# Padding the low key halves to 128 rows, a planner that keeps TensorE in one mode, and values of two units in one 512-column projection

## The chip, the cores and the metric

The kernel runs on one core of one Trainium2 chip. The metric is the device time of one execution in microseconds (us). The program is one launch; its inputs are the packed weights and tables, its output the final hidden state.

## The reference

Two layers of an encoder with 512 tokens of width 1024. Each layer normalises `x`, projects it with one wide matrix `w_in`, runs three branches on the pieces, and merges them:

```python
h = rms_norm(x, norm_w[i])
(qa, ka, va, ga, qb, kb, vb, gb, xbc, z, dt_raw, ua, ub, uc) = [h @ w for w in jnp.split(w_in[i], split_idx, axis=1)]
ya = neighbourhood_attention(qa, ka, va, na_rpb[i])   # 16 heads of 64, windows of 8 rows x 16 columns on a 8 x 64 grid
ya = (ya * jax.nn.silu(ga)) @ w_oa[i]
yb = dilated_mixture(rotary(qb), rotary(kb), vb)      # 24 heads in 3 groups of dilation 1, 4, 16, mixed by their log-sum-exp
yb = (yb * jax.nn.silu(gb)) @ w_ob[i]
yc = mamba2_bidirectional(xbc, z, dt_raw, ...) @ w_oc[i]   # 24 heads, chunks of 128, both directions
merged = jax.nn.sigmoid(ua) * ya + jax.nn.sigmoid(ub) * yb + jax.nn.sigmoid(uc) * yc
x = x + merged @ w_out[i]
gate = jax.nn.sigmoid(rms_norm(x, ple_norm_w[i]) @ w_ple_gate[i])
x = x + (p[i] @ w_ple[i]) * gate
```

The last line of the reference is `rms_norm(x, final_norm_w)`. All arithmetic is float32.

## The kernel before

**Precision.** TensorE multiplies in a reduced float32 format (`F32R`), so every operand of a projection is split into a high and a low part: `whi` and `wlo` for weights, `hh` and `hl` for the hidden state. `mm3` makes one product of three matmuls (high-high, high-low, low-high). A weight block of 128 x 1024 is fetched into `raw` by the SP queue; `block` makes `whi` on ScalarE and `wlo` on VectorE. Buffers: three each of `raw`, `whi`, `wlo`.

**Units.** `run` walks a list of steps in `ORDER`: `N0` to `N3` are the neighbourhood attention in units of four heads (`na_unit`), `S0` to `S3` the state-space groups of three head pairs (`ssm_group`, `ssm_pair`), `O0` and `O1` the two halves of the product with `w_oc` (`out_c`), `G` the gate on it, `D0` and `D1` the dilated attention in halves (`dil_half`), `A` and `B` the merges, `L` some stores. Then comes `tail`.

**Scores.** `stack` puts a head's query high part and low part on top of each other in `qs` (128 rows: 64 high, 64 low), and its key high part twice in `ks`; the key's low part goes into `kl`, where the heads of a pair hold 64 rows each. `scores` then needs, per head and half, one matmul `sc<-ks,qs` over 128 rows and one `sc<-kl,qs` over the head's own 64 rows. There are 192 of each. After the softmax, `turn` transposes the probabilities (`tr`), and matmuls into `av` multiply them with the values; an output there has 64 columns a head, in float32, which the profile shows as two passes.

**Values.** `vproj` projects 256 value columns with matmuls of 256 columns and two `pj` banks. `vproj_wide` does 512 columns with four banks (two `pj`, one `tr`, the one `av`); before, only `dil_half` uses it. `na_unit` writes the values to a scratch tensor `vd` and gathers windows of it into `vw`. PSUM has 3 `pj`, 2 `sc`, 2 `tr` banks and 1 `av` bank.

**What sets the order.** The code records all instructions as nodes, in the order of the steps. `schedule` then plans every engine's queue with a list planner: it takes the ready node with the lowest number on each engine, as far as 2500 nodes ahead of the first open one, if its tiles fit into the pools (`fits`), and it prices nodes by `cost`. The order that results is what the engines run; each runs its queue in order. All instructions are issued from one line of `emit` (L261 in the profile of before), so groups in the profile are told apart by the names of tiles.

Of the kernel before, what the change touches and what calls it, by code (L numbers as in the profile page):

```python
# [120 lines left out]
class Node:  # L121
    __slots__ = ("i", "eng", "method", "args", "kw", "tiles", "pred", "succ", "cost", "new", "dma", "table", "fetch", "issue",
                 "npred", "ready", "done", "rank")
# [27 lines left out]
def cost(n, eng):  # L151
# [11 lines left out]
    if eng == "tensor":  # L163
        if n.method == "transpose":
            return 107.0
        if lazy[1].base.dtype == F32R:
            return (0.418 * free + 13.5) * (0.6 if lazy[1].box[0][1] == 64 else 1.0)
        if out.box[0][1] <= 64:
            return 54.0 if out.box[0][0] >= 64 else 1.72 * max(free, 64)
        if lazy[1].box[0][1] == 64:  # L170
            return 240.0
# [21 lines left out]
class Recorder:  # L193
# [28 lines left out]
    def add(self, eng, method, args, kw):  # L222
        n = Node()
        n.i, n.eng, n.method, n.args, n.kw = len(self.nodes), eng, method, args, kw
        n.dma = method == "dma_start"
        n.fetch = n.dma and isinstance(kw["out"], Lazy) and kw["out"].base.pool.space != "DRAM"
# [8 lines left out]
        for group, wr in ((rest, False), (outs, True)):  # L235
            for ap in group:
# [11 lines left out]
                h.append((n, ap.box, wr))  # L248
        n.issue = 625.0 if n.dma and any(scattered(v) for v in (kw["out"], kw["in_"])) else 450.0
# [4 lines left out]
        self.nodes.append(n)  # L254

# [7 lines left out]

    WINDOW = 2500
    AHEAD = 600

    def schedule(self):
# [16 lines left out]
        seen = set()  # L284
        for n in nodes:
            n.new = []
            n.npred = len(n.pred)
            n.ready = 0.0
            for m in n.pred:
                m.succ.append(n)  # L290
            for t, wr in n.tiles.items():
                t.left += 1
                if t not in seen:
                    seen.add(t)
                    if t.tag:
                        n.new.append(t)
        avail = {q: [] for q in self.QUEUE}
        wait = {q: [] for q in self.QUEUE}
        for n in nodes:
            if n.npred == 0:  # L300
                for e in FLEX.get(n.eng, (n.eng,)):
                    heapq.heappush(avail[e], n.i)
# [3 lines left out]
        table, drain = None, False  # L306
# [3 lines left out]
        while len(order) < len(nodes):  # L310
# [3 lines left out]
            for q in avail:  # L314
# [3 lines left out]
                while w and w[0][0] <= now:  # L318
                    heapq.heappush(av, heapq.heappop(w)[1])
                skipped, n = [], None  # L320
                while av:
                    i = av[0]
                    if i > front + self.WINDOW:
# [4 lines left out]
                    if not (nodes[i].dma and i > front + self.AHEAD) and self.fits(nodes[i], free, front):  # L328
                        n = nodes[i]
# [4 lines left out]
                for i in skipped:  # L334
                    heapq.heappush(av, i)
# [7 lines left out]
                for t in n.new:  # L343
                    free[t.tag] -= 1
                    self.live[t.tag][front:n.i] += 1
# [8 lines left out]
                else:  # L354
# [37 lines left out]
    def fits(self, n, free, front):  # L392

        if not n.new:
            return True
        need = {}
        for t in n.new:
            need[t.tag] = need.get(t.tag, 0) + 1
        for k, v in need.items():
            if free[k] < v or (front < n.i and self.live[k][front:n.i].max() + v > self.caps[k]):  # L400
                return False
        return True

# [9 lines left out]
class Emit:  # L413
# [18 lines left out]
    NT = 55  # L432
# [17 lines left out]
    def block(self, spec, ncols):  # L450
# [5 lines left out]
        nc.scalar.copy(hi[:, :ncols], raw[:, :ncols])  # L456
        nc.vector.tensor_sub(lo[:, :ncols], raw[:, :ncols], hi.bitcast(F32)[:, :ncols])
# [42 lines left out]
    def vproj_wide(self, cols):  # L500
# [76 lines left out]
    def constants(self):  # L577
# [15 lines left out]
        self.eps = c(C_EPS, 1)  # L593

# [41 lines left out]
    def norm_h(self):  # L636
# [7 lines left out]
        for k in range(8):  # L644
# [4 lines left out]
            nc.scalar.copy(self.hh[k][:, S:576], self.hh[k].bitcast(F32)[:, 0:64])  # L649
            nc.scalar.copy(self.hl[k][:, S:576], self.hl[k].bitcast(F32)[:, 0:64])  # L650
# [236 lines left out]
    def dil_half(self, hf):  # L887
# [4 lines left out]
        far = self.vproj_wide([VB + 512 * g + 256 * hf for g in (1, 2)])  # L892
# [76 lines left out]
    def scores(self, pair, q, k, kl):  # L969


# [421 lines left out]
```

## Time and profile before

| | |
|---|---|
| median of three runs | 2452.09 us (2450.15 to 2454.11) |
| profiled execution | 2453.53 us, span 2451.6 us |
| mean granted TensorE clock | 0.982 |
| busy: TensorE, VectorE, ScalarE, GpSimd | 2350.0, 1642.3, 1122.5, 215.0 us |
| TensorE instructions | 12480 |
| HBM traffic | 272.74 MB, 111 GB/s mean |

The span is the time from the first to the last instruction of the profiled execution. PE is TensorE's matmuls, PEld its weight loads, DVE VectorE, ACT ScalarE, POOL GpSimd, SP the queue that fetches weights. A name such as `pj<-hh,whi` reads: out `pj`, moving operand `hh`, stationary operand `whi`. The form `64*128 64x256` means 64 rows and 128 columns of the array, and 256 columns that move. Matmuls overlap in the pipeline, so the recorded duration of one is longer than the step from its start to the next one's.

### The profile page before, as it was taken

Reading aid. Unit: us, or ns where it says so; the run is one execution under the profiler, and the core shown is the slowest. Engines: PE = TensorE matmul, PEld = TensorE weight load, DVE = VectorE, ACT = ScalarE, POOL = GpSimd, SP = SyncE. Lnnn points to the kernel's source line nnn. Section 1 sums busy time; section 2 is a strip of 40 time slices with the busy share of each in tenths; the row PEclk is TensorE's granted clock in tenths of the full one; section 3 lists DMA queues with packets and bytes.
Section 4 is the critical chain, followed back from the end, with each engine's and each line's share of the span. In section 5 each row is a group of like instructions: output and inputs, shape, how many; then the busy total and the mean of one; then the engine's idle time right before and its main releaser. Section 6 shows DMA issues by size and latency. Waiting matters only on the chain. (4 is left out here: it accounts for less than half of the span.)

```text
span 2451.6 us, 33345 instructions
## 1 busy us (share of the span) xinstructions
PE 2350.0 (96%) x12480; PEld 1928.1 (79%) x12480; DVE 1642.3 (67%) x3227; ACT 1122.5 (46%) x2148; POOL 215.0 (9%) x380
## 2 busy tenths in 40 slices
PE   7999899989998999999999998999899989999998
PEld 6677788878877877788877777788788778777888
DVE  6797978784465556535687878797735663665357
ACT  5636354433355445324465453644234554562245
POOL 1202020000001000200021110210000020002000
PEclk9999999999999999999999999999999999999999
DMA  6625252423214221533355442523322242116333
GB/s 229 162 88 164 86 149 76 136 80 103 86 61 104 89 78 61 172 116 105 109 170 145 117 142 90 148 88 113 101 93 71 73 124 76 66 61 170 107 110 129
DMA packets 111377, 272.74 MB, mean 111 GB/s; under 512 B 39360, under 2 KB 45984, under 8 KB 111216
## 3 DMA queue, kind: packets, MB, share of 16 engines
q1 hardware_dynamic: 56464, 189.73, 23.4%
q0 software_dynamic: 50400, 76.69, 11.8%
q10 hardware_dynamic: 4352, 4.20, 0.5%
q8 instruction: 98, 1.61, 0.3%
q14 instruction: 63, 0.52, 0.1%
HBM read 257.08 MB, written 13.21 MB: 110 GB/s over the span
## 5 line engine op out<-in xcount | busy, mean ns | idle before, releaser
L261 PE MATMUL pj<-hh,whi 128*128 128x512 f32 x1744 | 700.4, 402 | 3.8 <-ACT hh L261 3.8
L261 PE MATMUL pj<-hl,whi 128*128 128x512 f32 x1744 | 700.7, 402 | 1.4 <-DVE hl L261 1.4
L261 PE MATMUL pj<-hh,wlo 128*128 128x512 f32 x1728 | 693.1, 401 | 8.6 <-DVE wlo L261 8.6
L261 ACT CAST whi<-raw 128x1024 fp32r<-128x1024 f32 (+2 forms) x360 | 368.1, 1024 | 702.2 <-PE pj L261 545.2
L261 DVE TENSOR_TENSOR wlo<-raw,whi 128x1024 fp32r<-128x1024 f32 (+2 forms) x358 | 425.7, 1191 | 377.5 <-ACT whi L261 372.5
L261 PEld LDWEIGHTS pj<-hl,whi 128*128 128x128 f32 x1744 | 330.6, 190 | 79.9 <-issue 8.8
L261 PEld LDWEIGHTS pj<-hh,whi 128*128 128x128 f32 x1744 | 331.0, 190 | 78.4 <-issue 7.0
L261 PEld LDWEIGHTS pj<-hh,wlo 128*128 128x128 f32 x1728 | 326.9, 189 | 83.5 <-DVE wlo L261 10.2
L261 PE MATMUL pj<-yh,wlo 128*128 128x512 f32 (+1 forms) x576 | 213.3, 372 | 0.6 <-DVE wlo L261 0.6
L261 PE MATMUL pj<-yl,whi 128*128 128x512 f32 (+1 forms) x576 | 212.7, 370 | 0.0
L261 PE MATMUL pj<-yh,whi 128*128 128x512 f32 (+1 forms) x576 | 211.9, 369 | 0.6 <-ACT th L261 0.6
L261 PE MATMUL pj<-whi,hh 128*128 128x256 f32 (+1 forms) x448 | 139.4, 314 | 11.0 <-ACT th L261 7.1
L261 PE MATMUL pj<-wlo,hh 128*128 128x256 f32 (+1 forms) x448 | 139.7, 313 | 6.6 <-DVE wlo L261 6.6
L261 PE MATMUL pj<-whi,hl 128*128 128x256 f32 (+1 forms) x448 | 138.2, 311 | 0.0
L261 PEld LDWEIGHTS pj<-yh,wlo 128*128 128x128 f32 x576 | 109.9, 191 | 19.8 <-DVE wlo L261 1.4
L261 PEld LDWEIGHTS pj<-yh,whi 128*128 128x128 f32 x576 | 109.6, 190 | 18.6 <-ACT th L261 1.5
L261 PEld LDWEIGHTS pj<-yl,whi 128*128 128x128 f32 x576 | 109.5, 190 | 17.9 <-issue 0.3
L261 DVE SCALAR_TENSOR_TENSOR cv<-cx,cwh,cv 128x510 f32<-128x510 f32 (+1 forms) x160 | 119.3, 746 | 5.5 <-ACT cv L261 4.2
L261 PEld LDWEIGHTS pj<-whi,hh 128*128 128x128 f32 x448 | 96.0, 215 | 15.9 <-ACT th L261 8.4
L261 PEld LDWEIGHTS pj<-wlo,hh 128*128 128x128 f32 x448 | 97.5, 218 | 9.3 <-DVE wlo L261 8.3
L261 ACT ACTIVATE p<-p,nm 128x128 f32<-128x128 f32 (+2 forms) x192 | 80.1, 420 | 39.6 <-DVE nm L261 39.6
L261 PEld LDWEIGHTS pj<-whi,hl 128*128 128x128 f32 x448 | 97.4, 218 | 0.5 <-issue 0.3
(214 smaller groups left out, 3476.5 us busy)
## 6 DMA issues: line engine op xcount, KB each, us to landing
raw<-wt SPq DMA_DIRECT2D x322, 512.0 KB, 3.3
nb<-nab POOLq DMA_DIRECT2D x32, 384.0 KB, 4.6
af<-acd POOLq DMA_DIRECT2D x48, 256.0 KB, 6.0
ab<-acd POOLq DMA_DIRECT2D x48, 256.0 KB, 6.2
raw<-wt SPq DMA_DIRECT2D x32, 384.0 KB, 3.0
eb<-ead POOLq DMA_DIRECT2D x48, 192.0 KB, 9.6
vw<-vd POOLq DMA_DIRECT2D x56, 128.0 KB, 5.0
f<-fd POOLq DMA_DIRECT2D x24, 256.0 KB, 12.8
```

The costliest lines, as they stand in the source:

```text
L261: getattr(getattr(self.real, n.eng), n.method)(*[f(a) for a in n.args], **{k: f(v) for k, v in n.kw.items()})
```

## The change

Seven edits come together.

1. `kl` becomes a tile per head of 128 rows (`keylow`, two fixed pairs used in turn) whose other 64 rows are zeroed once. `scores` multiplies it over 128 rows, with the same `qs` as for `ks`, and finishes one head before the next.
2. `na_unit` projects the values of two units together with `vproj_wide` in the even unit; `vproj_wide` takes the tokens as an argument.
3. `ORDER` has `N3` between `S3` and `O1`, where it stood between `D0` and `D1`.
4. The planner gives each TensorE node a mode (`half` for 64 rows, `pair` for 64-column outputs, `wide` for the reduced format, `full` for float32). It looks past up to `STAY` = 12 ready nodes of another mode for one of the present mode, if that one is at most `NEAR` = 60 numbers behind.
5. The nodes are taken by rank: the two splits of a weight block count as 300 numbers earlier (`EARLY`), readers of PSUM on other engines as 60 earlier (`DRAIN`). The planner's prices for some matmuls and for a change of mode differ.
6. The copies of the first 64 columns of `hh` and `hl` to their end move from `norm_h` to the step `L` (`stores`).
7. The pool of general tiles has 51 buffers instead of 55; four tiles of that size are the `keylow`.

```diff
-            return (0.418 * free + 13.5) * (0.6 if lazy[1].box[0][1] == 64 else 1.0)
+            return 111.0 if lazy[1].box[0][1] == 64 else 0.418 * free + 13.5
...
-            return 240.0
+            return 136.0
...
+        n.split = False
+        n.drain = eng != "tensor" and any(isinstance(v, Lazy) and v.base.pool.space == "PSUM"
+                                          for v in list(args) + list(kw.values()))
...
+        n.mode = None
+        if eng == "tensor":
+            w = args[1]
+            n.mode = ("half" if w.box[0][1] == 64 else "pair" if args[0].box[0][1] == 64 else
+                      "wide" if w.base.dtype == F32R else "full")
...
+        return n
...
+    EARLY = 300
+    DRAIN = 60
+    STAY, NEAR = 12, 60
...
+            n.rank = n.i - (self.EARLY if n.split else self.DRAIN if n.drain else 0)
...
-                    heapq.heappush(av, heapq.heappop(w)[1])
-                skipped, n = [], None
+                    i = heapq.heappop(w)[1]
+                    heapq.heappush(av, (nodes[i].rank, i))
+                skipped, n, held, tries = [], None, [], 0
...
-                    i = av[0]
-                    if i > front + self.WINDOW:
+                    r, i = av[0]
+                    if r > front + self.WINDOW:
...
-                        n = nodes[i]
+                        if q == "tensor" and nodes[i].mode != mode and tries < self.STAY:
+                            if n is None or nodes[i].rank < n.rank:
+                                n = nodes[i]
+                            tries += 1
+                            held.append(i)
+                            continue
+                        if n is None or nodes[i].mode == mode and r < n.rank + self.NEAR:
+                            n = nodes[i]
+                        else:
+                            held.append(i)
...
-                for i in skipped:
-                    heapq.heappush(av, i)
+                for i in skipped + [i for i in held if n is None or i != n.i]:
+                    heapq.heappush(av, (nodes[i].rank, i))
...
-                        half = n.cost in (54.0, 1.72 * 128)
-                        c += 84.0 if drain and not half else 0.0
-                        drain = half
+                        c += 0.0 if n.mode == mode else 45.0 if {n.mode, mode} == {"wide", "full"} else 95.0
+                        mode = n.mode
...
-    NT = 55
+    NT = 51
...
-        nc.scalar.copy(hi[:, :ncols], raw[:, :ncols])
-        nc.vector.tensor_sub(lo[:, :ncols], raw[:, :ncols], hi.bitcast(F32)[:, :ncols])
+        for n in (nc.scalar.copy(hi[:, :ncols], raw[:, :ncols]),
+                  nc.vector.tensor_sub(lo[:, :ncols], raw[:, :ncols], hi.bitcast(F32)[:, :ncols])):
+            n.split = True
...
-    def vproj_wide(self, cols):
+    def vproj_wide(self, cols, tokens):
...
-                    lh, ll = self.hh[k][:, t:S:4], self.hl[k][:, t:S:4]
+                    lh, ll = self.hh[k][:, tokens[t]], self.hl[k][:, tokens[t]]
...
+        self.nkey = 0
+        self.keylow = [[self.cp.tile([128, S], F32R, name=f"kl{i}_{h}") for h in range(2)] for i in range(2)]
+        for pair in self.keylow:
+            for h in range(2):
+                self.nc.gpsimd.memset(pair[h].bitcast(F32)[64 - 64 * h:128 - 64 * h], 0.0)
...
-            nc.scalar.copy(self.hh[k][:, S:576], self.hh[k].bitcast(F32)[:, 0:64])
-            nc.scalar.copy(self.hl[k][:, S:576], self.hl[k].bitcast(F32)[:, 0:64])
...
 
-
         nc = self.nc
...
                 nc.tensor.matmul(sc[h][:, ii], q(h, pair, ii), k(h, pair, ii), start=ii == 0, stop=False)
-        for ii in range(2):
-            for h in range(2):
-                own = slice(64 * h, 64 * h + 64)
-                nc.tensor.matmul(sc[h][:, ii], q(h, pair, ii)[own], kl(pair, ii, own), start=False, stop=ii == 1)
+            for ii in range(2):
+                nc.tensor.matmul(sc[h][:, ii], q(h, pair, ii), kl(h, pair, ii), start=False, stop=ii == 1)
         return sc
...
-                             lambda b, ii, own: kl[own, keys(2 * b + ii)])
+                             lambda h, b, ii: kl[h][:, keys(2 * b + ii)])
...
         nc = self.nc
-        vn = self.vproj("w_in", VA + 256 * u, [slice(128 * t, 128 * t + 128) for t in range(4)])
-        vd = self.dp.tile([S, 256], F32, tag="vd", bufs=2, name=self.name("vd"))
-        for j in range(2):
-            nc.scalar.dma_start(out=vd[256 * j:256 * j + 256].rearrange("(t p) d -> p t d", p=128), in_=vn[j])
-        vg = vd.rearrange("(r c) d -> r c d", c=64)
+        if u % 2 == 0:
+            vn = self.vproj_wide([VA + 256 * u, VA + 256 * u + 256], [slice(128 * t, 128 * t + 128) for t in range(4)])
+            self.vd = self.dp.tile([S, 512], F32, tag="vd", bufs=2, name=self.name("vd"))
+            for t in range(4):
+                nc.scalar.dma_start(out=self.vd[128 * t:128 * t + 128], in_=vn[t].rearrange("p g d -> p (g d)"))
+        vg = self.vd.rearrange("(r c) d -> r c d", c=64)[:, :, 256 * (u % 2):256 * (u % 2) + 256]
         V = {}
...
-        kl = self.t(dtype=F32R, nm="kl")
+        kl = self.keylow[self.nkey % 2]
+        self.nkey += 1
...
-                eng.tensor_sub(kl[a], kp[a], ks[h].bitcast(F32)[a])
+                eng.tensor_sub(kl[h][a], kp[a], ks[h].bitcast(F32)[a])
...
-                nc.vector.scalar_tensor_tensor(kl[a], kp[a], scale, ks[h].bitcast(F32)[a], ALU.mult, ALU.subtract)
+                nc.vector.scalar_tensor_tensor(kl[h][a], kp[a], scale, ks[h].bitcast(F32)[a], ALU.mult, ALU.subtract)
...
+        nc = self.nc
+        for h in self.hh + self.hl:
+            nc.scalar.copy(h[:, S:576], h.bitcast(F32)[:, 0:64])
...
-    ORDER = ("N0 L S0 N1 S1 N2 S2 O0 S3 O1 G D0 N3 D1 A B",
-             "N0 L S0 N1 S1 N2 S2 O0 S3 O1 G D0 N3 D1 A B")
+    ORDER = ("N0 L S0 N1 S1 N2 S2 O0 S3 N3 O1 G D0 D1 A B",
+             "N0 L S0 N1 S1 N2 S2 O0 S3 N3 O1 G D0 D1 A B")
```

Three places show what that does to the order. The names in the rows are out<-moving,stationary for TensorE and out<-inputs elsewhere; the last column is the shape of the out, and buffer numbers are part of the names.

First, TensorE in N0 of the first layer, at the outputs of the first pair's second half. Before:

```order
L261 MATMUL pj_786<-hl_283,whi_596 128x512
L261 MATMUL pj_786<-hh_270,wlo_613 128x512
L261 MATMUL av_798<-pt_829,vw_559 64x128
L261 MATMUL pj_786<-hh_281,whi_596 128x512
L261 MATMUL av_798<-pt_838,vw_559 64x128
L261 MATMUL av_798<-pt_829,vw_602 64x128
L261 MATMUL av_798<-pt_838,vw_602 64x128
L261 MATMUL av_798<-pt_829,vw_578 64x128
L261 MATMUL av_798<-pt_838,vw_578 64x128
L261 MATMUL av_798<-pt_829,vw_578 64x128
L261 MATMUL av_798<-pt_838,vw_578 64x128
L261 MATMUL pj_786<-hl_289,whi_596 128x512
```

And now:

```order
L270 MATMUL pj_802<-hh_320,whi_651 128x512
L270 MATMUL av_853<-pt_887,vw_625 64x128
L270 MATMUL av_853<-pt_893,vw_625 64x128
L270 MATMUL av_853<-pt_887,vw_665 64x128
L270 MATMUL av_853<-pt_893,vw_665 64x128
L270 MATMUL av_853<-pt_887,vw_646 64x128
L270 MATMUL av_853<-pt_893,vw_646 64x128
L270 MATMUL av_853<-pt_887,vw_646 64x128
L270 MATMUL av_853<-pt_893,vw_646 64x128
L270 MATMUL pj_802<-hl_356,whi_651 128x512
```

The eight outputs stood as one and seven with a projection between them, and now stand together. Over the whole program the stretches of `av` outputs of 64 columns number 191 before and 149 now, of which those of a single output 89 and 66 (others of seven: 69 and 63); stretches of transposes number 254 and 225, single ones 126 and 84. The 192 matmuls `sc<-kl` stand in 68 stretches of two and 14 of four before.

Second, TensorE at the last head pair of S3 in the first layer; `tr<-consts,cv` is its transpose, `sc<-cx` the first matmul on the result, `pj<-yh` and `pj<-yl` are O1's projections. Before:

```order
L261 MATMUL pj_4828<-yl_3863,whi_4800 128x512
L261 MATMUL tr_4837<-consts_114,cv_4764 128x128 x4
L261 MATMUL sc_4861<-cx_4857,tT_4442 128x128 x3
L261 MATMUL sc_4866<-cx_4859,tT_4442 128x128 x3
L261 MATMUL pj_4812<-yh_3851,wlo_4868 128x512
L261 MATMUL pj_4812<-yh_4044,whi_4661 128x512
```

Now the transpose stands 17 projection rows of N3 ahead of `sc<-cx`; the last of them and what follows:

```order
L270 MATMUL pj_4775<-hh_315,whi_4632 128x512
L270 MATMUL pj_4775<-hl_351,whi_4632 128x512
L270 MATMUL pj_4775<-hh_315,wlo_4649 128x512
L270 MATMUL sc_4819<-cx_4812,tT_4413 128x128 x3
L270 MATMUL sc_4826<-cx_4816,tT_4413 128x128 x3
L270 MATMUL pj_4775<-hh_320,whi_4632 128x512
```

N3's projections `pj<-hh` and `pj<-hl` now fill the place that was empty between the two. For all 24 head pairs of the S groups the projections between the transpose and `sc<-cx` number 0 to 12 before and 7 to 17 now.

Third, VectorE behind D0 in the first layer, where D0's outputs `o` are multiplied with factors `f` that come back from a scratch tensor. Before, N3's low keys stand among them:

```order
L261 TENSOR_TENSOR o_5957<-o_5957,f_6875 128x512
L261 TENSOR_TENSOR wlo_6914<-raw_6832,whi_6901 128x1024
L261 TENSOR_TENSOR o_6057<-o_6057,f_6885 128x512
L261 SCALAR_TENSOR_TENSOR kl_6934<-pj_6853,ks_6912 64x512
L261 TENSOR_TENSOR o_5957<-o_5957,o_6057 128x512
```

Now it is D1 that follows, and its blocks stand there:

```order
L270 TENSOR_TENSOR wlo_7229<-raw_7004,whi_7221 128x1024
L270 TENSOR_TENSOR o_6331<-o_6331,f_7236 128x512
L270 TENSOR_TENSOR wlo_7270<-raw_7195,whi_7260 128x1024
L270 TENSOR_TENSOR o_6437<-o_6437,f_7244 128x512
L270 TENSOR_TENSOR o_6584<-o_6584,f_7251 128x512
L270 TENSOR_TENSOR o_6331<-o_6331,o_6437 128x512
```

`wlo_7229` is the last low half of D1's far values, ahead of the first product with `f`; `wlo_7270`, behind it, is the block that D1 needs after them. No low key stands between the products any more.

More of the change, by code (lines that the diff above doesn't have):

```diff
@@ L121 @@
 class Node:
-    __slots__ = ("i", "eng", "method", "args", "kw", "tiles", "pred", "succ", "cost", "new", "dma", "table", "fetch", "issue",
-                 "npred", "ready", "done", "rank")
+    __slots__ = ("i", "eng", "method", "args", "kw", "tiles", "pred", "succ", "cost", "dma", "table", "fetch", "issue",
+                 "npred", "ready", "done", "rank", "split", "drain", "mode")
 LATENCY = {"PE": {"PE": 0.0, "*": 197.0}, "ACT": {"ACT": 63.0, "PE": 271.0, "POOL": 159.0, "*": 142.0},
@@ L283, in schedule @@
         assert not over, over
-        seen = set()
+        self.first, self.placed = first, set()
         for n in nodes:
-            n.new = []
             n.npred = len(n.pred)
+            n.rank = n.i - (self.EARLY if n.split else self.DRAIN if n.drain else 0)
             n.ready = 0.0
@@ L292, in schedule @@
                 t.left += 1
[L293 to L296, printed above, removed]
         avail = {q: [] for q in self.QUEUE}
@@ L301, in schedule @@
                 for e in FLEX.get(n.eng, (n.eng,)):
-                    heapq.heappush(avail[e], n.i)
+                    heapq.heappush(avail[e], (n.rank, n.i))
         clock = dict.fromkeys(self.QUEUE, 0.0)
@@ L305, in schedule @@
         dge = dma = now = 0.0
-        table, drain = None, False
+        table, mode = None, None
         events, order = [], []
@@ L342, in schedule @@
                 n.cost = cost(n, q)
-                for t in n.new:
+                for t in self.new(n):
+                    self.placed.add(t)
                     free[t.tag] -= 1
-                    self.live[t.tag][front:n.i] += 1
+                    self.live[t.tag][front:first[t]] += 1
                 if n.dma:
@@ L392, in fits, with new @@
     def fits(self, n, free, front):
[L394 to L397, printed above, removed]
+        need, until = {}, {}
+        for t in self.new(n):
             need[t.tag] = need.get(t.tag, 0) + 1
+            until[t.tag] = max(until.get(t.tag, 0), self.first[t])
         for k, v in need.items():
-            if free[k] < v or (front < n.i and self.live[k][front:n.i].max() + v > self.caps[k]):
+            if free[k] < v or (front < until[k] and self.live[k][front:until[k]].max() + v > self.caps[k]):
                 return False
         return True
+    def new(self, n):
+        return [t for t in n.tiles if t.tag and t not in self.placed]
 class RecEngine:
@@ L891, in dil_half @@
         near = self.vproj("w_in", VB + 256 * hf, [slice(64 + 128 * t, 192 + 128 * t) for t in range(4)])
-        far = self.vproj_wide([VB + 512 * g + 256 * hf for g in (1, 2)])
+        far = self.vproj_wide([VB + 512 * g + 256 * hf for g in (1, 2)], [slice(t, S, 4) for t in range(4)])
         val = lambda g, t: far[t][:, g - 1] if g else near[t // 2][:, t % 2]
@@ L1150, in na_pair @@
             sc = self.scores(b, lambda h, b, jj: q[h][:, 256 * b + 128 * jj:256 * b + 128 * jj + 128],
-                             lambda h, b, jj: win(k[h], 2 * b + jj), lambda b, jj, own: win(kl[own], 2 * b + jj))
+                             lambda h, b, jj: win(k[h], 2 * b + jj), lambda h, b, jj: win(kl[h], 2 * b + jj))
             mx = self.small((128, 2, 2), "nmx")
```

## The prediction

> **What bounds the kernel now.** I read the page first: the span, the busy time of each engine. TensorE is the bound.
>
> ```profile
> span 2451.6 us, 33345 instructions
> PE 2350.0 (96%) x12480; PEld 1928.1 (79%) x12480; DVE 1642.3 (67%) x3227; ACT 1122.5 (46%) x2148; POOL 215.0 (9%) x380
> ```
>
> So PE idles 2451.6 - 2350.0 = 102 us, and a gain has to come out of that or out of the 2350. The view of PE's waits comes next (engine, line, who is waited for: total us, times, longest). Short waits on VectorE lead it, among them one on the low key tile `kl` and one on `cx` of an S group; the 9.3 is the first load.
>
> ```profile
> PE pj L261 <- DVE wlo L261: 15.8, 13, 3.4
> PE sc L261 <- DVE kl L261: 12.6, 4, 5.1
> PE pj L261 <- ACT whi L261: 9.3, 1, 9.3
> PE sc L261 <- DVE cx L261: 8.5, 6, 3.2
> ```
>
> Where they lie is seen in the table by windows (window, length, then busy us of PE, PEld, DVE, ACT and POOL, granted clock, DMA share, GB/s). The second row is group S3 with the start of O1, the third the end of D0 with the start of N3, the last S3 of the second layer; the first is the layer's start.
>
> ```profile
> 27.00:37.00 10.00, 6.88 (x19) 3.57 (x20) 9.90 (x16) 7.59 (x24) 0.00 (x0) 0.81 0.15 50
> 460.00:540.00 80.00, 73.39 (x377) 59.45 (x376) 69.04 (x128) 29.50 (x49) 5.53 (x15) 0.94 0.25 82
> 755.00:815.00 60.00, 52.95 (x290) 44.73 (x287) 40.81 (x88) 33.06 (x71) 12.42 (x19) 0.91 0.50 125
> 1668.00:1750.00 82.00, 75.26 (x386) 61.05 (x386) 69.61 (x128) 29.49 (x49) 5.54 (x15) 0.94 0.27 86
> ```
>
> In the last three PE idles 6.6, 7.1 and 6.7 us at a lower clock, so the two places cost some 27 of the 102 in two layers. PE's timeline (start, duration) is the last view: a matmul's recorded duration overlaps the next one's, so I price everything by steps from start to start.
>
> **The padded lows.** One score head of N1 in that timeline:
>
> ```profile
> 233.33 0.40 PE L261 MATMUL pj<-hh,whi 128*128 128x512 f32 x1
> 233.56 0.40 PE L261 MATMUL sc<-ks,qs 128*128 128x256 f32 x2
> 233.89 0.50 PE L261 MATMUL sc<-kl,qs 64*128 64x256 f32 x2
> 234.32 0.50 PE L261 MATMUL pj<-hl,whi 128*128 128x512 f32 x1
> 234.66 0.40 PE L261 MATMUL pj<-hh,wlo 128*128 128x512 f32 x1
> 234.89 0.40 PE L261 MATMUL pj<-hh,whi 128*128 128x512 f32 x1
> ```
>
> A 512-column projection steps 0.23 (234.66 to 234.89). From 233.33 to 234.66 is 1.33 us; without two projections 0.87 us remain for two `ks` and two `kl`: two `kl` of 64 rows need 0.43, and the projection after them 0.34 instead of 0.23. A 256-column matmul of 128 rows steps 0.12:
>
> ```profile
> 315.22 0.28 PE L261 MATMUL pj<-whi,hl 128*128 128x256 f32 x1
> 315.34 0.28 PE L261 MATMUL pj<-whi,hh 128*128 128x256 f32 x1
> ```
>
> Padded to 128 rows, two `ks` and two `kl` are four of these, 0.48 us, which saves 0.39. In the order of before the 192 `kl` stand in 68 visits of two and 14 of four; now none changes the row count. 68 x 0.39 = 26.5 us. The visits of four, where two heads share the array, I put at 0.15 each: 2 us, between 0 and 4. Term: 28 us. No row shows the padded form itself; the bounds are 24 (each of the 192 at 0.14) and 31. The padding costs POOL four memsets once, and `kl` is now one of two fixed pairs: a pair's writes wait for the scores of the pair but one before, which lie a whole pair back.
>
> The Trainium skill, page "TensorEngine Tiling (Array Packing)", sections Theoretical Speedup and Key Properties, promises up to twice the speed for a contraction of 64 rows and says that changing the tiling mode drains TensorE. The first half speaks against padding: by it two `kl` would take 0.12 us now, padding would lose, and the time would be that of the second rival below, 2416. The trace agrees with the second half (0.43 for two, and 0.11 more behind them).
>
> **Fewer mode changes.** The attention and S outputs (`av`, 64 columns) are also a mode of their own:
>
> ```profile
> 83.49 0.40 PE L261 MATMUL pj<-hh,wlo 128*128 128x512 f32 x1
> 83.82 0.43 PE L261 MATMUL av<-pt,vw 128*64 128x128 f32 x2
> 84.18 0.49 PE L261 MATMUL pj<-hh,whi 128*128 128x512 f32 x1
> 84.61 1.09 PE L261 MATMUL av<-pt,vw 128*64 128x128 f32 x14
> 85.62 0.50 PE L261 MATMUL pj<-hl,whi 128*128 128x512 f32 x1
> 85.96 0.39 PE L261 MATMUL pj<-hh,wlo 128*128 128x512 f32 x1
> ```
>
> And a visit of sixteen passes in the second layer's N0:
>
> ```profile
> 1323.21 1.09 PE L261 MATMUL av<-pt,vw 128*64 128x128 f32 x16
> 1324.24 0.49 PE L261 MATMUL pj<-hl,whi 128*128 128x512 f32 x1
> ```
>
> Going in costs 0.10 (0.33 instead of 0.23), leaving 0.11 (85.62 to 85.96), and a visit with one output (x2, since each is two passes) holds PE 0.36: 0.57 in all. Sixteen passes together take 1.03, fourteen 1.01, so a lone output joined to its seven is free. The order has 191 such visits before and 149 now, lone ones 89 and 66. 23 x 0.57 = 13 us; the other 19 lose at least both changes, 0.21, at most 0.57; I take 0.3, as most are groups that stay as long: 6 us. Term: 19 us, from 9 (42 x 0.21) to 24.
>
> Transposes are batched too (254 visits become 225), which I cost at nothing:
>
> ```profile
> 701.81 0.27 PE L261 MATMUL tr<-consts,p 128*128 128x128 f32 x1
> 701.84 0.48 PE L261 MATMUL pj<-hh,wlo 128*128 128x512 f32 x1
> 702.15 0.27 PE L261 MATMUL tr<-consts,p 128*128 128x128 f32 x1
> ```
>
> A lone transpose and a projection step 0.34, 0.11 above the projection, about the transpose's own work. If each lone one lost 0.1, 3 us.
>
> **Values of two units together.** 768 matmuls of 256 columns become 384 of 512: 768 x 0.12 = 92 us against 384 x 0.23 = 88. Term: 4 us, between 0 and 6. The weight blocks stay four a pair, and the ACT queue still writes four pieces of `vd`, earlier for the odd unit. The projection now holds one `tr` bank and the only `av` bank, so N2's begins under S1's last outputs; the order lets those outputs (the lone one, then seven) go ahead of it.
>
> **N3 ahead of O1, and the waits.** S3's last pair stands at the end with only O1 to fill in:
>
> ```profile
> 519.98 0.66 PE L261 MATMUL tr<-consts,cv 128*128 128x128 f32 x4 [1.26 <-DVE cv L261]
> 523.85 2.90 PE L261 MATMUL sc<-cx,tT 128*128 128x128 f32 x12 [3.21 <-DVE cx L261]
> 534.19 1.24 PE L261 MATMUL av<-z,tT 128*64 128x128 f32 x14 [1.85 <-DVE z L261]
> ```
>
> From transpose to `cx` takes 3.9 us, with no projection between; now 17 stand there, 17 x 0.23 = 3.9 us. I take the 6.3 us of the three rows as gone, 12.6 in both layers. N3 behind D0 stalled on `kl`, because VectorE, in order, held it behind a product with `f`:
>
> ```profile
> 795.14 0.69 DVE L261 TENSOR_TENSOR o<-o,f 128x512 f32<-128x512 f32 x1 [2.78 <-DMA f<-fd]
> 795.86 0.68 DVE L261 SCALAR_TENSOR_TENSOR kl<-pj,ks 64x512 fp32r<-64x512 f32 x1
> 796.60 0.79 PE L261 MATMUL sc<-kl,qs 64*128 64x256 f32 x2 [5.08 <-DVE kl L261]
> 797.32 0.79 PE L261 MATMUL pj<-hh,whi 128*128 128x512 f32 x1
> 797.91 0.63 PE L261 MATMUL pj<-hl,whi 128*128 128x512 f32 x1
> 798.34 0.63 PE L261 MATMUL pj<-hh,wlo 128*128 128x512 f32 x1
> ```
>
> Now D1 follows D0, and its far values (96 x 0.23 = 22 us, all of whose low halves stand ahead of the `f` product on VectorE) cover that. I take 5.1 us, 10 in two layers. After such a stall a projection steps 0.43 (797.91 to 798.34), half speed. A mean clock of 0.91 over 60 us is 10.8 us at half clock; less the 7.1 idle, 3.7 us of work took twice its time, 1.9 us lost; in S3's window (9.6 - 6.6) / 2 = 1.5. Both layers: 7 us. Sum of the waits: 12.6 + 10 + 7 = 30. Late next is VectorE, with S3's and N3's work side by side: in S3's window it is busy 69.04 of 80 already. I give 5 back: term 25, from 0 (all waits return elsewhere) to 50 (the earlier low halves and PSUM reads, which the new ranks bring, also take a third of the 66 us of idle time that neither these places nor the first load make). N3's DMAs (`nb`, `vw` on POOL's queue, weights on SP's) move from a window with a DMA share of 0.50 to one with 0.25, past S3's broadcasts on POOL's queue and away from the `f` broadcast.
>
> **The rest at nothing.** Small copies of `hh` and `hl` leave the layer's start:
>
> ```profile
> L261 ACT CAST hh<-hh x16: 241/244/247, 27.6 to 1247.1; 128x64 fp32r<-128x64 f32 x16
> ```
>
> A layer has 8 of them and 8 of `hl`, 16 x 0.24 = 3.9 us of ScalarE, but VectorE is busy 9.90 of 10 us there (row 27 to 37); it hides them, 0 to 2 us. Four tiles fewer in the pool are the four that `kl` now owns. The prices in the planner cost no time by themselves.
>
> Sum: 28 + 19 + 4 + 25 = 76 us. The profiled execution took 2453.5 us (span 2451.6), 1.4 above the median of 2452.1: 2453.5 - 76 = 2377.5, and 2376 against the median.
>
> **Rivals.** First, the waits only move: VectorE becomes the bound of the S groups. For it:
>
> ```profile
> 93.00:170.00 77.00, 69.17 (x370) 54.58 (x369) 70.96 (x149) 35.85 (x68) 6.83 (x11) 0.98 0.32 95
> ```
>
> It is busy 92% of S0's window, more than PE. Then the 25 is lost and perhaps 10 more: 2401 to 2411. Against it: N3's light VectorE work is spread into S3. Second, packing: if two `kl` were worth 0.12 together once visits are kept whole, padding adds 96 x 0.12 = 11.5 us instead of saving 28: 2376 + 39.5 = 2416. The rows speak against it, since even visits of four pay the change. (It is the first half of the Trainium skill's rule named above, page "TensorEngine Tiling (Array Packing)", Theoretical Speedup.) Third, slower: the planner passes up to 12 ready instructions of another mode; if that holds back the S pairs' transposes, `cx` and outputs, the engine that has no slack there starves PE. Both layers have 24 S pairs; 76 / 24 = 3.2 us a pair, as long as the longest such wait today (3.21), cancels the gain, and 4.5 us a pair give 2376 + 24 x 4.5 = 2484. The order speaks against it: 7 to 17 projections stand between transpose and `cx` where 0 to 12 stood. Fourth, the planner's order changes nothing on the chip: the rows of PE's order differ already.
>
> **The numbers.** Forecast 0.76; waits move 0.13; packing 0.05; slower 0.03; no net change 0.03. The time is the forecast's, 2376. Smallest gain 24 + 9 + 0 + 0 = 33 gives 2419, largest 31 + 24 + 6 + 50 = 111 gives 2341. I take 2342 to 2412, which reaches into the first rival. Within 0.2% (5 us), about what a measurement here can tell, needs 71 us or more to be lost: 0.03. Faster 0.94, slower 0.03.
>
> **What would show it.** Right: `sc<-kl` reads 128 rows, x192, and the projection behind it steps 0.23; PE's waits on `kl` nearly vanish and those on `cx` halve; the granted clock around S3 and behind D0 is near 1; PE's busy time falls by some 50 us and its idle time by some 25. Wrong: padded `kl` stepping 0.2, a wait on `wlo` at the start of D1, waits on `z`, `cx` or `cv` in S0 to S2 above those of before, or PE waiting for `tr` or `av` banks in N0 and N2.

## The result and the profile after

The changed kernel took 2342.4 us (median; 2340.4 to 2345.2), the kernel before 2453.1 beside it: ratio 0.955, 95% interval 0.953 to 0.957. That is 110 us less, where 76 were forecast. The median lies 0.4 us inside the lower end of the range (2342 to 2412), and two of the four executions (2340.4 and 2340.7) lie below it. The page's span and busy times:

```profile
span 2342.9 us, 32733 instructions
PE 2282.3 (97%) x12096; PEld 1880.5 (80%) x12096; DVE 1643.4 (70%) x3227; ACT 1112.8 (47%) x2132; POOL 219.1 (9%) x384
```

TensorE (PE) is busy 67.7 us less (2350.0 before) and idle 2342.9 - 2282.3 = 60.6 us, 41.0 less than the 101.6 before. The mean granted clock is 0.991, where it was 0.982. In both traces the clock is granted in full or by half and nothing between: at half for 90.4 us before and for 40.9 us now. Read by windows over these stretches, PE is busy in them for 69.4 and 24.2 us; a projection steps 0.43 there instead of 0.23, about twice its time, so by estimate half of it, 34.7 and 12.1 us, was lost, and 22.6 of the 67.7 us are this loss grown smaller. The view of PE's waits (engine, line, who is waited for: total us, times, longest):

```profile
PE tr L270 <- DVE np L270: 14.0, 2, 7.1
PE pj L270 <- ACT whi L270: 6.6, 1, 6.6
PE av L270 <- ACT pt L270: 4.7, 6, 1.0
PE sc L270 <- ACT ks L270: 4.1, 2, 2.3
```

The waits that led before, on `wlo` (15.8), `kl` (12.6), `cx` (8.5), `th` (7.7) and `cv`, are gone or below 2 us. A new one leads: two waits of 7 us on `np`, N0's normalised probabilities. The table by windows (window, length, busy us of PE, PEld, DVE, ACT and POOL, granted clock, DMA share, GB/s) shows the places of the prediction: the start, S3 with N3 beside it, the end of D0 with D1's start, and S3 of the second layer.

```profile
27.00:37.00 10.00, 6.75 (x15) 4.87 (x16) 9.91 (x16) 7.28 (x24) 0.00 (x0) 0.50 0.43 159
440.00:520.00 80.00, 80.00 (x418) 65.96 (x417) 68.06 (x122) 35.64 (x57) 4.97 (x8) 1.00 0.33 105
780.00:850.00 70.00, 65.56 (x341) 58.34 (x340) 46.21 (x75) 34.57 (x68) 7.19 (x10) 0.98 0.33 99
1600.00:1680.00 80.00, 79.31 (x416) 65.32 (x415) 71.13 (x127) 36.54 (x57) 6.15 (x10) 1.00 0.31 100
```

PE is busy 80.00 of 80 us in S3 at full clock, where it was 73.39 at 0.94, with VectorE as busy as before. The start of the layer has gained nothing: PE is busy 6.75 of 10 us there (6.88 before), at a clock of 0.50 where it was 0.81. PE's timeline (start, duration) shows why S3 closed and what a score head costs now:

```profile
220.23 0.40 PE L270 MATMUL sc<-ks,qs 128*128 128x256 f32 x2
220.47 0.40 PE L270 MATMUL sc<-kl,qs 128*128 128x256 f32 x2
220.71 0.40 PE L270 MATMUL pj<-hh,whi 128*128 128x512 f32 x1
220.95 0.39 PE L270 MATMUL pj<-hl,whi 128*128 128x512 f32 x1
...
507.36 0.60 PE L270 MATMUL tr<-consts,cv 128*128 128x128 f32 x4
507.72 0.47 PE L270 MATMUL pj<-hl,whi 128*128 128x512 f32 x1
...
511.48 0.39 PE L270 MATMUL pj<-hh,wlo 128*128 128x512 f32 x1
511.70 1.50 PE L270 MATMUL sc<-cx,tT 128*128 128x128 f32 x12
...
525.82 1.09 PE L270 MATMUL av<-z,tT 128*64 128x128 f32 x14
```

Two `ks` and two padded `kl` take 220.23 to 220.71, 0.48 us, and the projection behind them steps 0.24. From the transposes of S3's last pair to its `cx` PE has 17 projections and no wait; before it waited 3.21 us there. The last row is the last output of that pair.

One execution of the kernel e1_nt51 in the table below, the one that was profiled, took 4969.7 us where the other four took 2494.3 to 2499.1; the cause is not known, its ratio goes by the four, and its busy times are left out.

### The profile page after: what moved, and what is told of

It reads as the page before. It is cut to its first block, busy times and chain, and to the rows that moved or that the text cites. A ratio compares the mean times of both kernels' runs of the same rounds, so it can differ in the third digit from the quotient of the medians.

```text
span 2342.9 us, 32733 instructions
## 1 busy us (share of the span) xinstructions
PE 2282.3 (97%) x12096; PEld 1880.5 (80%) x12096; DVE 1643.4 (70%) x3227; ACT 1112.8 (47%) x2132; POOL 219.1 (9%) x384
## 5 line engine op out<-in xcount | busy, mean ns | idle before, releaser
L270 PE MATMUL pj<-hl,whi 128*128 128x512 f32 x1744 | 693.3, 398 | 2.1 <-DVE hl L270 2.1
L270 PE MATMUL pj<-hh,whi 128*128 128x512 f32 x1744 | 693.0, 397 | 1.5 <-ACT hh L270 1.5
L270 PEld LDWEIGHTS pj<-yh,whi 128*128 128x128 f32 x576 | 108.6, 189 | 17.5 <-issue 0.7
L270 PE MATMUL pj<-whi,hh 128*128 128x512 f32 (+1 forms) x256 | 88.7, 348 | 2.0 <-ACT v L270 2.0
L270 PE MATMUL pj<-whi,hl 128*128 128x512 f32 (+1 forms) x256 | 87.6, 342 | 0.8 <-DVE hl L270 0.8
L270 PE MATMUL pj<-wlo,hh 128*128 128x512 f32 (+1 forms) x256 | 87.8, 343 | 0.0
L270 ACT ACTIVATE np<-np,nnm 128x256 f32<-128x256 f32 x128 | 63.7, 499 | 48.9 <-DVE nnm L270 48.9
L270 ACT COPY pt<-tr 128x512 f32<-128x512 f32 x128 | 71.2, 579 | 26.3 <-PE tr L270 25.2
L270 POOL DMA_DIRECT2D af<-acd x48 | 28.4, 591 | 483.3 <-DVE y L270 224.5
```

Source lines behind the costliest of these rows:

```text
L270: getattr(getattr(self.real, n.eng), n.method)(*[f(a) for a in n.args], **{k: f(v) for k, v in n.kw.items()})
```

## The experiments

PE busy and idle are from each kernel's page (idle is span less busy), clock is the mean granted one. us are medians.

| kernel | us | ratio to before (95%) | PE busy | PE idle | clock |
|---|---|---|---|---|---|
| before | 2453 to 2456 | 1 | 2350.0 | 101.6 | 0.982 |
| after | 2342.4 | 0.9551 (0.9534 to 0.9567) | 2282.3 | 60.6 | 0.991 |
| e1_pad: before, padded `kl` alone | 2472.3 | 1.0070 (1.0058 to 1.0083) | 2334.8 | 135.7 | 0.974 |
| e1_nt51: before, 51 tiles | 2499.0 | 1.0169 (1.0152 to 1.0187) | - | - | - |
| e6_fix: after, 64-row `kl`, same order | 2369.8 | 0.9642 (0.9620 to 0.9664) | 2315.5 | 51.9 | 0.992 |
| e2_nomode: after, no mode preference | 2346.6 | 0.9560 (0.9548 to 0.9572) | 2284.5 | 59.1 | 0.993 |
| e3_norank: after, ranks off | 2417.2 | 0.9843 (0.9828 to 0.9857) | 2302.1 | 108.2 | 0.983 |
| e3a_noearly: after, splits' rank off | 2430.2 | 0.9887 (0.9866 to 0.9908) | 2311.7 | 121.1 | 0.979 |
| e4_n3late: after, N3 behind D0 | 2402.2 | 0.9785 (0.9772 to 0.9797) | 2290.0 | 108.6 | 0.981 |
| e9_neither: after, ranks off, N3 behind D0 | 2469.3 | 1.0053 (1.0036 to 1.0070) | 2317.2 | 152.0 | 0.974 |
| e10_plan: new planner, old data path | 2388.9 | 0.9729 (0.9712 to 0.9745) | 2317.0 | 70.4 | 0.989 |
| e10_nt51: the same, 51 tiles | 2374.1 | 0.9667 (0.9645 to 0.9689) | 2313.4 | 58.6 | 0.991 |
| e5_narrow: after, narrow values | 2360.6 | 0.9597 (0.9571 to 0.9622) | 2289.9 | 69.9 | 0.990 |
| e8_late6: after, later landing planned | 2329.3 | 0.9481 (0.9462 to 0.9501) | 2277.4 | 51.6 | 0.994 |

Below, differences are those of the ratios, times 2453 us.

### What the padding is worth

**e1_pad**, before with the padded lows alone:

```diff
-    NT = 55
+    NT = 51
...
-                nc.tensor.matmul(sc[h][:, ii], q(h, pair, ii)[own], kl(pair, ii, own), start=False, stop=ii == 1)
+                nc.tensor.matmul(sc[h][:, ii], q(h, pair, ii), kl(h, pair, ii), start=False, stop=ii == 1)
...
-        kl = self.t(dtype=F32R, nm="kl")
+        kl = self.keylow[self.nkey % 2]
...
```

> The kernel before with the padded kl alone (two fixed pairs of 128-row low key tiles, four tiles fewer in the pool); order rules, values and unit order stay as before. Theory (a padded kl is priced like a ks, as the step sum had it): sc<-kl steps 0.12 us, PE busy falls by 25 to 32 us, idle time within 8 us of before, time 2453 - 28 = 2425 (2418 to 2432). Rival (most of the 110 us is the padding, since the mode change of a 64-row visit costs more than its steps show): 2390 or less. Rival (packing): two 64-row kl were worth 0.12 us together, padding alone costs: 2460 to 2465.

It came out 17 us slower, which none of the three had: PE's busy time fell by 15.2, where 25 to 32 were forecast, and idle time rose by 34.1. At half the clock PE is busy 95.9 us here, 69.4 before: 13.2 us more are lost to it, and without them the busy time falls by 28.4, as forecast. Its waits, and the end of S3 in its timeline (in brackets the idle time before the row and who ended it):

```profile
PE pj L261 <- DVE wlo L261: 29.5, 13, 6.9
PE av L261 <- DVE z L261: 18.0, 8, 3.4
PE sc L261 <- DVE kl L261: 10.6, 3, 4.7
```

```profile
526.99 1.09 PE L261 MATMUL av<-z,tT 128*64 128x128 f32 x14 [3.17 <-DVE z L261]
...
550.08 0.79 PE L261 MATMUL pj<-yh,wlo 128*128 128x512 f32 x1 [6.83 <-DVE wlo L261]
```

The wait on `kl` itself did not grow (12.6 before), so the two fixed pairs don't bind. S groups wait for `z`, and O1 for `wlo`: the order changed. Either the four tiles fewer or the planner's price of a longer `kl` did that.

**e1_nt51**, before with `NT = 51` and nothing else:

> The kernel before with 51 tiles in the pool instead of 55 and nothing else. In e1_pad the padded kl stepped as forecast and PE's busy time fell, but idle time rose by 34 us. Theory (four tiles fewer hold back the S groups, whose z, wlo and cv were waited for): 20 us or more slower, 2475 to 2490, with waits on z and wlo as in e1_pad. Rival (the planner's price of the padded kl moved the order): 2448 to 2458.

41 us slower: four tiles fewer alone cost more than e1_pad lost, and put on top of them, the padding saves 1.0169 - 1.0070, 24 us.

**e6_fix**, the changed kernel with the same order and tiles, `kl` sliced:

```diff
-                getattr(getattr(self.real, n.eng), n.method)(*[f(a) for a in n.args],
+                getattr(getattr(self.real, n.eng), n.method)(*[f(a) for a in n.swap or n.args],
...
+                own = slice(64 * h, 64 * h + 64)
+                n.swap = (n.args[0], q(h, pair, ii)[own], kl(h, pair, ii)[own])
```

The planner sees the padded operands, and the sliced ones are issued.

> The changed kernel, its order of instructions and its tiles unchanged, but each sc<-kl matmul reads only its 64 rows (q and kl sliced to the head's own half). Nothing else moves, so this is the price of the padding alone, without the planner. Theory (the step sum): 96 visits of two, each 0.39 us longer, 37 us: 2379 (2368 to 2384), PE busy up by 30 to 40. Rival (a 64-row visit costs about what the padded one does, and e1_pad's 15 us of busy time came from elsewhere): 2340 to 2350.

22 us slower (27 by the medians), less than the theory's 37; PE's busy time is up by 33.2, as it had it (30 to 40). The same head in its timeline:

```profile
217.95 0.40 PE L271 MATMUL sc<-ks,qs 128*128 128x256 f32 x2
218.28 0.51 PE L271 MATMUL sc<-kl,qs 64*128 64x256 f32 x2
218.72 0.50 PE L271 MATMUL pj<-hh,whi 128*128 128x512 f32 x1
219.06 0.39 PE L271 MATMUL pj<-hl,whi 128*128 128x512 f32 x1
```

From `ks` to the second projection it takes 1.11 us against 0.72 with the padding: 0.39, the step sum's price to the hundredth; over all 96 visits the 33.2 us make 0.35 each. A quarter of it came back as idle time, which fell by 8.7, since a slower PE reaches its waits later (the `np` waits were 7.4 us in all instead of 14.0). The Trainium skill, page "TensorEngine Tiling (Array Packing)", Theoretical Speedup, allows up to twice the speed for 64 rows. In this order each head stands by itself, and two 64-row `kl` take 0.44 where two padded ones take 0.24. The kernel before shows the speedup where the heads of a pair stand together, in its 14 visits of four:

```profile
70.72 0.51 PE L261 MATMUL sc<-kl,qs 64*128 64x256 f32 x4
71.16 0.50 PE L261 MATMUL pj<-hh,whi 128*128 128x512 f32 x1
```

Four take 0.44 (70.72 to 71.16), as long as two alone. With the 0.11 that the projection behind them loses, that is 0.07 more than the 0.48 of four padded ones, where the prediction put 0.15. The page's other rule, that a change of the mode drains (Key Properties), agrees with these 0.11 us, paid at every visit.

### The planner's parts

**e2_nomode** (`STAY = 0` for 12):

> The changed kernel with the planner's preference for the present mode off (it passes 0 rows instead of 12); ranks, padding, wide values and unit order stay. The order then has 154 visits of av instead of 149 and 237 of transposes instead of 225. Theory (the ranks and the unit order made the visits fewer, not the preference): 5 x 0.57 + 12 x 0.1 = 4 us, 2344 to 2350. Rival (the preference is where the unforecast 34 us come from): 2365 or more.

2346.6 us, within the theory's range; the interval overlaps that of the changed kernel: the preference for a mode is not where the gain is.

**e3_norank** (`EARLY = 0` for 300, `DRAIN = 0` for 60):

> The changed kernel with both ranks at zero (the weight splits are no longer taken 300 rows early, nor the reads of PSUM 60 rows early); all else stays. Theory (the ranks took away the waits on wlo, 15.8 us, on th, 7.7, and the half clock behind them, which the sum had only in its bound): 15 to 30 us slower than the changed kernel, 2357 to 2372, with waits on wlo back above 10 us. Rival (the unit order alone took the waits): 2338 to 2348.

72 us slower, more than twice the theory's most: 47.6 us more of idle time and 19.8 more of busy time. PE is busy 63.1 us at half the clock instead of 24.2, which alone makes 19.5 of the 19.8. The waits on `wlo`, `nmx` and `cv` of the kernel before are back, and others:

```profile
PE pj L270 <- DVE wlo L270: 16.3, 9, 4.4
PE sc L270 <- DVE nmx L270: 13.0, 8, 2.6
PE sc L270 <- ACT ks L270: 12.2, 12, 3.7
PE tr L270 <- DVE cv L270: 11.8, 8, 3.0
```

Its VectorE timeline shows how a `wlo` comes late: the weight split (1.22 us) stands in a row of S0's operations, the last two of them shown, with no idle time ahead of it, and PE waits 4.10 us for it.

```profile
170.37 0.74 DVE L270 SCALAR_TENSOR_TENSOR cv<-cx,cwh,cv 128x510 f32<-128x510 f32 x1
171.03 0.68 DVE L270 TENSOR_TENSOR z<-z,af 128x512 f32<-128x512 f32 x1
171.63 1.22 DVE L270 TENSOR_TENSOR wlo<-raw,whi 128x1024 fp32r<-128x1024 f32 x1
```

```profile
172.90 0.79 PE L270 MATMUL pj<-hh,wlo 128*128 128x512 f32 x1 [4.10 <-DVE wlo L270]
```

**e3a_noearly** (`EARLY = 0` alone):

> The changed kernel with the weight splits' rank at zero, the rank of the PSUM reads kept. Both ranks together were worth 75 us. Theory (the wait on wlo leads the waits of the kernel before, so most of the 75 is the splits' rank): 2390 to 2417, waits on wlo above 10 us. Rival (the reads of PSUM, which free the banks and end the waits on nmx, cv and z, are most of it): 2342 to 2365, no wait on nmx above 4 us.

82 us slower than the changed kernel, beyond the theory's range (waits on `wlo`: 17.9 us), and 11 slower than with both ranks off. So the early reads of PSUM gain nothing without the early splits. Whether the splits' rank alone would do as well as both was not run.

**e4_n3late** (`ORDER` of before):

```diff
-    ORDER = ("N0 L S0 N1 S1 N2 S2 O0 S3 N3 O1 G D0 D1 A B",
+    ORDER = ("N0 L S0 N1 S1 N2 S2 O0 S3 O1 G D0 N3 D1 A B",
...
```

> The changed kernel with N3 behind D0 again, as in the kernel before; all else stays. Theory (N3 ahead of O1 is worth the waits at S3 and behind D0 with their half clock, 30 us less 5): 2342 + 25 = 2367 (2358 to 2372), idle time 15 to 20 us above the changed kernel's, the granted clock at S3 below 0.96. Rival (the ranks alone take those waits): 2342 to 2350.

57 us slower, again over twice the theory: 48.0 us more of idle time and 7.7 more of busy time, which is what the half clock makes (39.5 us busy in it instead of 24.2). S3 with O1's start and D0's end with N3, by windows:

```profile
460.00:540.00 80.00, 62.02 (x336) 50.31 (x335) 65.43 (x127) 27.15 (x45) 7.37 (x18) 0.89 0.20 63
755.00:820.00 65.00, 54.85 (x335) 46.29 (x334) 45.01 (x101) 36.01 (x79) 8.33 (x12) 0.89 0.31 86
```

PE idles 18.0 and 10.2 us there, more than the kernel before did in the same places (6.6 and 7.1). PE's timeline and VectorE's:

```profile
508.03 0.66 PE L270 MATMUL tr<-consts,cv 128*128 128x128 f32 x4
...
528.67 1.97 PE L270 MATMUL av<-z,tT 128*64 128x128 f32 x14 [8.38 <-DVE z L270]
534.73 1.65 PE L270 MATMUL pj<-yh,whi 128*128 128x512 f32 x3 [4.09 <-ACT yh L270]
```

```profile
523.46 0.55 DVE L270 TENSOR_TENSOR eb<-eb,sc 128x384 f32<-128x384 f32 x1 [3.12 <-DMA eb<-ead]
...
527.93 0.69 DVE L270 TENSOR_TENSOR z<-z,af 128x512 f32<-128x512 f32 x1
```

VectorE, in order, waits for a broadcast `eb` ahead of the product `z` on which S3's last output hangs. From the transposes of the last pair to that output it takes 20.6 us (508.03 to 528.67), and in the changed kernel 18.5 (507.36 to 525.82). In the kernel before it took 14.2 (519.98 to 534.19). So N3 doesn't make the chain short; it fills it. Without N3 nothing is left but O1, and that needs this very output.

**e9_neither** (the two edits together):

> The changed kernel with both ranks at zero and N3 behind D0, so padding, wide values and the mode preference alone stay of the change. The kernel without the ranks lost 75 us and the one without N3's place 60. Theory A (ranks and unit order cover the same stalls, each is enough for none of them alone): about as slow as either, 2400 to 2425. Theory B (they act on different stalls and add up): 2342 + 75 + 60 = 2477, slower than the kernel before. Theory C (any other order than the changed kernel's is some 60 us worse, whatever it leaves out): 2395 to 2425 too, but with waits in other places than the two it combines.

123 us slower than the changed kernel; 72 and 57 apart make 129. So the two add up, as theory B has it: the ranks are worth 66 us without N3's place and 72 with it, N3's place 52 without the ranks and 57 with them. What is left of the change (padding, wide values, the preference, the planner's new prices) makes no faster kernel at 51 tiles: 13 us slower than before. Against e1_pad its busy time is 17.6 lower and its idle time 16.3 higher: the work that they save there turns into waiting.

**e10_plan**, the new planner on the old data path (64-row `kl`, narrow values, 55 tiles):

> The changed kernel's planner (ranks, mode preference, unit order) with the data path of before: 64-row kl of one tile, both heads together, narrow values, 55 tiles. Theory (the planner's part is all of the gain that is not padding 28 and values 4): 2342 + 32 = 2374 (2365 to 2385), idle time near the changed kernel's 60. Rival (planner and data path need each other): 2400 or more, with idle time back near 100.

66 us faster than before, between the two theories: 33.0 of busy and 31.2 of idle time.

**e10_nt51**, the same with 51 tiles:

> The planner's part on the old data path (e10_plan) with 51 tiles in place of 55. Under the planner of before four tiles cost 45 us. Theory (the new ranks and unit order keep fewer tiles alive, so the same four tiles cost next to nothing): 2383 to 2396. Rival (the tiles cost the same under either planner, and the changed kernel would gain 45 with room for them): 2425 to 2440.

15 us faster than with 55, outside both theories. Four tiles fewer cost 41 us under the old planner and gain 15 under the new one. A price of memory alone would have one sign; what changes with the tiles is the order that the planner finds (e10_nt51 has another TensorE instruction than e10_plan at 538 of 12480 places, by names without buffer numbers, and e1_nt51 another than the kernel before at 700). Which of these places costs the time was not traced.

**e5_narrow**, the changed kernel with narrow values:

```diff
-        if u % 2 == 0:
-            vn = self.vproj_wide([VA + 256 * u, VA + 256 * u + 256], [slice(128 * t, 128 * t + 128) for t in range(4)])
...
+        vn = self.vproj("w_in", VA + 256 * u, [slice(128 * t, 128 * t + 128) for t in range(4)])
...
```

> The changed kernel with the values of each neighbourhood unit projected by themselves again, 768 matmuls of 256 columns for 384 of 512; all else stays. Theory (4 us, 0 to 6, by the steps): 2342 + 4 = 2346 (2342 to 2350). Rival (the wide form carries the gain left over between the planner's part and the padding, some 15 us, since it also frees the values' banks and drops an av visit's neighbour): 2352 to 2360.

11 us by the ratios (18 by the medians; its runs spread from 2348 to 2363): busy time 7.6 more, idle 9.3 more. Of the 7.6, 4.6 are half clock (33.3 us busy in it instead of 24.2); the 3.0 that remain fit the step sum's 4. The whole is more than that, and the interval doesn't tell the rival's 15 from 8.

### A faster version

The `np` waits have their cause in VectorE's timeline of the changed kernel:

```profile
91.62 0.69 DVE L270 TENSOR_TENSOR ab<-ab,acT 128x512 f32<-128x512 f32 x1 [1.52 <-DMA ab<-acd]
92.23 0.17 DVE L270 RECIPROCAL ndn<-ndn 128x4 f32<-128x4 f32 x1
97.81 0.69 DVE L270 TENSOR_TENSOR ab<-ab,acT 128x512 f32<-128x512 f32 x1 [5.41 <-DMA ab<-acd]
98.42 1.34 DVE L270 TENSOR_SCALAR np<-np,ndn 128x256 f32<-128x256 f32 x4
```

The reciprocal is done at 92.4, but `np` stands behind a product of S0 for whose broadcast VectorE waits 5.41 us. The planner takes ready instructions alone, so by its prices the broadcast had landed. **e8_late6** tells it otherwise:

```diff
                     n.done = dma + (910.0 if n.fetch else 1500.0)
+                    if q == "gpsimd" and any(m in ("partition_broadcast", "to_broadcast") for m, a, k in getattr(n.kw["in_"], "ops", ())):
+                        n.done += 6000.0
```

> The changed kernel with one price of the planner changed: broadcasts on POOL's queue are taken to land 6 us later, so that VectorE has N0's normalisation of np ahead of more of S0's products that wait for such a broadcast. Theory (PE's longest waits left, 7 us on np in N0 of each layer with half clock behind them, shrink): 10 to 18 us faster than the changed kernel, 2324 to 2332. Rival (another order brings other waits): 2342 or more.

2329.3 us, within the theory's range, and 0.9481 of before, clear of the changed kernel's interval. VectorE now has `np` ahead of the later `ab`:

```profile
88.67 0.66 DVE L270 TENSOR_TENSOR ab<-ab,acT 128x512 f32<-128x512 f32 x1
89.25 1.35 DVE L270 TENSOR_SCALAR np<-np,ndn 128x256 f32<-128x256 f32 x4
...
97.31 0.69 DVE L270 TENSOR_TENSOR ab<-ab,acT 128x512 f32<-128x512 f32 x1 [1.02 <-DMA ab<-acd]
```

No wait on `np` is left in PE's waits, and idle time is 9.0 lower.

## Why the prediction was right, and where it fell short

The parts can be read along two chains of kernels, each step one edit or a few. Both run from the kernel before to the changed one, so each adds up to the 110 us, within rounding, whatever its steps are.

| chain by the old planner first | us | chain by the new planner first | us |
|---|---|---|---|
| 55 to 51 tiles (e1_nt51) | +41 | ranks, preference, prices, unit order, copies (e10_plan) | -66 |
| padding (e1_pad) | -24 | 55 to 51 tiles (e10_nt51) | -15 |
| all but ranks and N3's place (e9_neither) | -4 | padding (e5_narrow) | -17 |
| N3 ahead of O1 (e3_norank) | -52 | wide values (after) | -11 |
| ranks (after) | -72 | | |

Four tiles alone move the time by 41 or 15 us, so a step between two kernels whose orders differ carries the planner's chance with it. Padding was measured in three settings, the ranks and N3's place in two each; the wide values in one.

- **Padding, 28 us: right.** 24, 17 and 22 us in three settings; of busy time without the half clock 28 (e1_pad), 23 (e10_nt51 to e5_narrow) and 32 (e6_fix); 0.39 at a head, as read from the steps. The packing rival did not come, though not because the two heads can't run side by side: in the visits of four they do, and the change of mode takes the gain back. What the term left out is that the four tiles that `kl` owns leave the pool: costed at nothing, they moved the order by 41 us one way or 15 the other.
- **Fewer mode changes, 19 us: somewhat large.** Of the 67.7 us of busy time 22.6 are half clock, 23 to 32 padding and 3 values; 11 to 19 remain for the visits, 14 with e1_pad's padding. From e1_pad to e9_neither, where all of the change comes in but the ranks and N3's place, it is 9 (17.6, less 5.4 of half clock and 3.0 of the values), and this came back as idle time. The preference is not what made the visits fewer: without it the outputs `av` stand in 154 instead of 149, where the kernel before has 191. Which other edit did was not measured apart.
- **Values, 4 us: right for the steps.** 3.0 of busy time; 11 us in all, with half clock and idle time.
- **Waits, 25 us: the step that fell short.** It has two parts, 18 of idle time (12.6 + 10 less 5) and 7 of half clock; the runs show 41 and 23, together 64, which is beyond the term's own bound of 50.
- The idle time: the 22.6 us of waits that the term named at S3 and behind D0 did go. Beside them the waits on `wlo` (15.8 to 0.4), `th` (7.7 to 0), the rest of `cv` (4.1) and `nmx` (5.1 to 1.7) went, 30.6 in all, in pieces of 0.3 to 3.4 us, and 14.0 on `np` came where 5 were given back: 39. e3_norank has those on `wlo`, `nmx` and `cv` back and e4_n3late, with the ranks, has not (0.9, 1.7 and 0), so it is the ranks that took them. They stood only in the bound.
- The half clock: the term took the idle time off the time at half clock, as if PE's idle time lay in it. In the traces half the clock comes mostly behind the wait, while PE works (69.4 of the 90.4 us before). At S3 and behind D0 in both layers the kernel before is busy 31.7 us at half clock, so 16 us were lost there, not 7; the other 7 of the 23 went elsewhere.
- **In sum**, the busy time fell by 67.7 (forecast 58, with the half clock) and the idle time by 41 (forecast 18). The miss of 34 is half clock (16 more) and idle time (23 more), less some 5 that the visits and the values fell short. That the time still lies in the range, by 0.4 us, is luck: the waits overran their bound, and padding, visits and values stayed below theirs (45 us of 61).
- **What to look for**: clock 1.00 at S3, `kl` at 128 rows with the next projection at 0.24, no wait on `kl` or `cx`: as named. Of the signs against it none came, but the one new wait was of the kind that the first rival has: VectorE's order, at N0 and not at S3. That rival (waits only move, 2401 to 2411) did not come, since VectorE is as busy beside N3 as before and PE has no wait there; the 2402 of e4_n3late lies in its range by chance, for there N3 is not beside S3. The slower rival (S pairs starving PE) didn't come either: PE's waits show none on `cv`, `cx` or `z`.

## What to carry to other kernels

Price a matmul form by start-to-start steps with its entry and exit: with the order held, 96 visits cost 33.2 us of busy time where that price gave 37. But where a planner sets the order, an edit that only takes four tiles can move more time than the edit it serves, so test it with the order held fixed and with the planner free, apart. In a kernel that one engine fills to 96%, add up all short waits, not only the long ones, and count the half clock behind them by the busy time in it; then ask which wait is covered by other work and which is merely moved. A planner that believes a DMA early puts a waiting instruction at the head of an in-order queue: compare its landing times with the trace before anything else.

## What the runs showed that was not expected

**A wait of 2.3 us is enough for half the clock.** PE's timeline of the changed kernel, at two waits:

```profile
543.81 0.43 PE L270 MATMUL av<-pt,vw 128*64 128x128 f32 x2 [1.04 <-ACT pt L270]
544.17 0.50 PE L270 MATMUL pj<-hh,wlo 128*128 128x512 f32 x1
544.51 0.40 PE L270 MATMUL pj<-hh,whi 128*128 128x512 f32 x1
...
837.68 0.79 PE L270 MATMUL sc<-ks,qs 128*128 128x256 f32 x2 [2.31 <-ACT ks L270]
838.27 0.63 PE L270 MATMUL sc<-kl,qs 128*128 128x256 f32 x2
...
840.40 0.63 PE L270 MATMUL pj<-hh,whi 128*128 128x512 f32 x1
840.83 0.51 PE L270 MATMUL pj<-hl,whi 128*128 128x512 f32 x1
841.17 0.39 PE L270 MATMUL pj<-hh,wlo 128*128 128x512 f32 x1
```

After 1.04 us nothing slows down; after 2.31 projections step 0.43 for some 3.3 us (to 841), which loses about 1.6 us more. The trace grants half the clock from 837.65 to 841.06, 3.41 us, and in each of thirteen traces such a stretch lasts 3.41 us or a multiple of it, but for the last, which the kernel's end cuts off. In these thirteen (all but e1_nt51's), after the first 30 us, no stretch of 3.41 us on this grid at full clock that held more than 1.91 us of PE idle time was followed by one at full clock, and of those followed by half the clock the least held 1.02. The Trainium skill, page "TensorE: Matmul & The Clock Gate", section "HAM oscillation — how this bites in real kernels", sets the limit at idle gaps over about 3.4 us; this wait was shorter and still cost it.

**Four tiles of a pool of 55 are worth +41 or -15 us**, with the same work on every engine.
